# A two-layer transformer trunk on one core: transposes of the norm in four banks, buffers of their own for four weight units, gate/up blocks opened token tile by token tile, down projection in halves

## The chip, the core and the metric

The kernel runs on one core of a Trainium2 chip. Its engines work side by side, each on its own list of instructions in order: TensorE (PE) multiplies matrices into PSUM, which has eight banks of 128 x 512 float32; VectorE (DVE) and ScalarE (ACT) work element by element and empty PSUM; GpSimd (POOL) does small arithmetic and issues some DMAs; SyncE (SP) issues the DMAs that fetch weights. Semaphores hold an instruction back until what it reads is there and what it overwrites is free. The metric is the device time of one execution in microseconds (us); less is better.

## The reference, cut to what matters

256 tokens of width 2048 pass through two layers. After the attention of a layer:

```
x   = layer_norm(ALPHA * x + concat(out_a, out_b) @ w_o, ln1_g, ln1_b)
ffn = (silu(x @ w_gate) * (x @ w_up)) @ w_down          # 2048 -> 5632 -> 2048
x   = layer_norm(ALPHA * x + ffn, ln2_g, ln2_b)
```

All of it is float32. The attention part (a sparse head group with an indexer, and a latent head group) is not touched by the change.

## The kernel before, in words

**Weights.** A weight unit is 256 rows (two k of 128) by 512 columns, 512 KB. `load_unit` (L313) has SP fetch it into a `raw` buffer (L302), ACT copy it rounded into `wh` (L309) and DVE write the rest, raw minus wh, into `wl` (L310). A product is three matmuls of 512 columns for each k: high x high, high x low, low x high. Units go through 5 pairs of wh/wl, and 2 more in the phase called "more"; raw has 4 buffers and 2 more (`some`, L291). That phase lasts from the last pass of the output projection through the FFN to the first projection chunk of the next layer.

**Tokens.** There are two token tiles of 128, t0 and t1. `proj` (L317) takes a unit and multiplies both token tiles by it: 12 matmuls.

**Last passes.** `last_pass` (L772) ends the output projection, and the down projection likewise: eight units (4 columns of 512, two units each) are loaded, all of t0 is finished, then all of t1, so the units have to stay. After t0, and again after t1, `then` starts the norm of that token tile: `moments` (L360, bn_stats on DVE, two small POOL steps), `normalise`, and for the norms whose result is multiplied again `norm_T` (L381): four chunks of four 128 x 128 transposes on PE, each chunk read by four ACT instructions that apply the gain and the shift, then a copy and a subtraction on DVE that give the operands `xh` and `xl`. The chunks take PSUM banks 4 and 5 in turn. `norm_T` is a task that the loops advance: `tick()` after each unit lets tasks whose waiting is over emit their next step. The last norm of layer two is `norm_out` (L421), which writes the output.

**Gate and up.** The first of eleven blocks of 512 hidden columns is plain (`gu`, L809). In the other ten, `gate_up` (L852) does four quads: a quad is gate and up for one unit u and its partner u + 4. Quads 0 and 1 are plain: 4 units, 48 matmuls. Quads 2 and 3 are `wino_quad` (L887), a Strassen-Winograd form: 4 raw loads, 4 additions of raw units on DVE (L893), 7 products of 6 matmuls, each of which needs its own wh and wl; their token operands s1 to s4 come from `sum_operands` (L815) out of sums and differences of chunks 1 and 3 of the normalised tokens. Banks: c11 (gate, t0) 4, c21 (gate, t1) 5, c12 and c22 (up) 6 and 7 as one tile, the products p1, p5, p6, p7 in 0 to 3. At the end of the last wino quad eight DVE and ACT instructions put gate and up together (L904 to L933). The order is plain 0, `between`, wino 2, plain 1, wino 3. `hidden` (L831) then does silu, product, transposes and split into `hT`.

**Down.** `down` (L945) multiplies the hidden blocks two at a time. `between` in block 2 runs it for blocks 0 and 1: 4 columns of 4 units, 192 matmuls; block 4 does it for 2 and 3, and so on. Blocks 1, 3, 5, 7, 9 and 10 have no down in them. At the end come blocks 8 and 9, and block 10 as the last pass. From the third block on, results are added to x by a DMA with addition that POOL issues (L963).

**Order.** The source is one stream of instructions. The framework's planner deals them out to the engines: for each engine it takes, at every moment of a simulated run, the ready instruction that stands first in the source. So PE can run a later product while an earlier one waits for its weights; what is fixed by the plan then runs in that order on the chip. Tiles of one tag share its buffers; an instruction that writes a new tile waits until a buffer is free. The tag a8 has ten buffers of 8 KB per partition, for x, xh, xl, hT and the attention's outputs.

Of the kernel before, what the change touches and what calls it, by code (L numbers as in the profile page):

```python
# [31 lines left out]
P = 128  # L32
# [26 lines left out]
HALF = NKT // KU // 2  # L59
T2 = 11  # L60
LASTU = 2
# [17 lines left out]
def hybrid_trunk(ctx: ExitStack, tc: tile.TileContext, x, xt_in, pos, w_in, g_cq, g_ckv, w_uq,  # L79
# [225 lines left out]
    def parts(raw, n):  # L305
        pool, bufs = some("n", UNITS, MORE)
        wh = pool.tile([P, KU * C], F32R, name=nm("wh"), tag="wh", bufs=bufs)
        wl = pool.tile([P, KU * C], F32R, name=nm("wl"), tag="wl", bufs=bufs)
# [72 lines left out]
    def norm_T(gbT, y, hi, lo, keep=None):  # L381


        for _ in normalise(y, moments(y)):
            pass
        yield 5
        for c in range(D // C):
            tp = trp()
            transpose4([y[:, c * C + i * P:c * C + (i + 1) * P] for i in range(4)], tp)
            if keep is not None and c in keep:  # L390
                v = keep[c]
            else:
                v = t2([P, 4, P], "v")
# [84 lines left out]
    def layer(l, xh, xl, norms, last):  # L478
# [292 lines left out]

        def last_pass(unit, ks, lhs, then):  # L772

            us = [[load_unit(unit(c, k), KU * C) for k in ks] for c in range(D // C)]
# [24 lines left out]
        ffn, kept = [True], []  # L799
        phase["held"] = True  # L800
        for t in range(NT):
            v = phase["pool"].tile([P, 2, 4, P], F32, name=nm("kept"), tag="raw", bufs=RAWMORE)
            kept.append({1: v[:, 0], 3: v[:, 1]})
# [11 lines left out]
        def sum_operands():  # L815

            a = [[kept[t][c] for c in (1, 3)] for t in range(NT)]
            for name, x, y in (("s1", a[1][0], a[1][1]), ("s2", a[0][0], "s1"), ("s3", a[1][0], a[0][0]),
                               ("s4", a[0][1], "s2")):
                y = sums[y][2] if isinstance(y, str) else y  # L820
                v = t2([P, 4, P], "sv")
                nc.vector.tensor_tensor(v, x, y, op=ALU.subtract)
                hi, lo = (phase["pool"].tile([P, 4, P], F32R, name=nm(name), tag=name + p, bufs=1) for p in "hl")
                split(hi, lo, v)
                sums[name] = hi, lo, v
            phase["held"] = False

        def slhs(name):
            return lambda k: tuple(m[:, k % 4, :] for m in sums[name][:2])
# [22 lines left out]
        def gate_up(fc, plain, wino, between):  # L852
# [26 lines left out]
            def plain_quad(u, lastz):  # L879
                for i, col in enumerate(("c11 c21", "c12 c22")):  # L880
                    for v in (u, u + HALF):
                        w = load_unit(w_gu[i][l, fc, v], KU * C)
                        for t, name in enumerate(col.split()):
                            passes(name, token(t), unit(v), w, lastz and name == "c22" and v != u)
                        tick()

            def wino_quad(u, final):  # L887
# [11 lines left out]

                lo_, hi_ = unit(u), unit(u + HALF)  # L900
                p("p1", token(0), r11, lo_)
                if final:
                    e = t2([P, C], "e")
                    nc.scalar.activation(e, o["p1"], AF.Copy)  # L904
                p("p2", token(0), r21, hi_)
                if final:
                    g0 = t2([P, C], "g0")
                    nc.vector.tensor_tensor(g0, e, o["c11"], op=ADD)
# [6 lines left out]
                if final:  # L915
                    nc.vector.tensor_tensor(e, o["p6"], e, op=ALU.subtract)
                tick()
                p("p7", slhs("s3"), r12, lo_)
                if final:
                    v = t2([P, C], "v7")  # L920
                    nc.vector.tensor_tensor(v, e, o["p7"], op=ADD)
                    nc.vector.tensor_tensor(e, e, o["p5"], op=ADD)
                add(r21, r11, r21)
# [14 lines left out]
            for i, (u, w) in enumerate(zip(plain, wino)):  # L938
                plain_quad(u, i == len(plain) - 1)
                if i == 0:  # L940
                    between()
                r = wino_quad(w, i == len(wino) - 1)
            return r

        def down(fcs, hTs, then):  # L945
# [4 lines left out]
            units = C // P // KU * len(fcs)  # L950
            u0 = C // P // KU * fcs[0]
            if fcs[-1] == NFC - 1:
                units -= LASTU
            for c in range(D // C):
                o = proj([(w_down[l, c, u0 + u], range(u * KU, (u + 1) * KU)) for u in range(units)], lhs, C)
# [8 lines left out]
            if fcs[-1] == NFC - 1:  # L964
                finish(*[h[2] for h in held])
                last_pass(lambda c, k: w_down[l, c, u0 + k // KU], [(units + i) * KU for i in range(LASTU)], lhs, then)

# [15 lines left out]
        def group():  # L983
            finish(*[h[2] for h in held])
            if len(held) == 2 and held[-1][0] < NFC - 2:
                down([h[0] for h in held], [h[1] for h in held], behind_ffn)
                held.clear()

        g = gu(0, 0, lambda: finish(*norms))
        sum_operands()  # L990
        affine(ln1_g[l], ln1_b[l], 0)
        u = gu(1, 0)
        affine(ln1_g[l], ln1_b[l], 1)
        spawn_hidden(0, g, u, free_banks)
        for fc in range(1, NFC):
            g, u = gate_up(fc, (0, 1), (2, 3), group)
# [5 lines left out]
        ffn[0] = False  # L1002
# [4 lines left out]
        finish(*[h[2] for h in held[:2]])  # L1007
        down([h[0] for h in held], [h[1] for h in held], behind_ffn)
# [59 lines left out]
```

## Time and profile before

| | |
|---|---|
| median of 3 runs | 2224.64 us (2223.5 to 2225.68) |
| profiled execution, its own time | 2223.74 us |
| its span, first to last instruction | 2221.9 us |
| PE, DVE, ACT, POOL busy | 2179.9, 1699.9, 1191.0, 109.0 us |
| granted TensorE clock | 0.998 of full speed over the span |
| weights and the rest read from HBM | 416.33 MB |

Busy time counts an engine's instructions. Matmuls overlap: of two in a row the second starts before the first ends, so PE shows as busy without a break while they follow each other, and idle only where one starts late.

### The profile page before, as it was taken

To read this page: it belongs to the slowest core of one execution; us is meant where nothing else is said; L and a number is where in the kernel's file an instruction comes from. 1 tells how busy PE (TensorE), PEld (TensorE's weight loads), DVE (VectorE), ACT (ScalarE), POOL (GpSimd) and SP (SyncE) were. 2 spreads that over 40 slices of the span, in tenths; PEclk is the share of its full clock that TensorE was granted. 3 is DMA by queue.
4 is the path that set the end of the run, shared out by engine and by line. 5 is a ranking of instruction groups with operands and counts; after the bars stand their busy time and mean duration, and the time that the engine had idled before them with its cause. 6 is when DMAs were issued, how large, how long until landed. Compare 5 with 4: busy or idle time off the path is not lost. (4 is left out here: it accounts for less than half of the span.)

```text
span 2221.9 us, 27847 instructions
## 1 busy us (share of the span) xinstructions
PE 2179.9 (98%) x10128; PEld 1800.6 (81%) x10128; DVE 1699.9 (77%) x2215; ACT 1191.0 (54%) x1537; POOL 109.0 (5%) x198
## 2 busy tenths in 40 slices
PE   8999999999999999999999999999999999999997
PEld 7888888788788787877878888877888888888885
DVE  6685556987968788699567757568879697887985
ACT  5555544554545555565455554445545555555562
POOL 0100000100010000100100000000000100000002
PEclk9999999999999999999999999999999999999999
DMA  8544455665576766666755455547655758577583
GB/s 304 165 159 162 153 168 171 230 213 175 200 216 209 230 195 227 194 208 208 207 160 172 155 173 180 172 156 246 220 176 203 221 191 242 177 249 208 196 275 105
DMA packets 126057, 437.04 MB, mean 197 GB/s; under 512 B 14320, under 2 KB 14368, under 8 KB 125664
## 3 DMA queue, kind: packets, MB, share of 16 engines
q1 hardware_dynamic: 113760, 409.26, 54.9%
q0 software_dynamic: 12160, 26.01, 5.8%
q8 instruction: 79, 1.29, 0.2%
q14 instruction: 58, 0.48, 0.1%
HBM read 416.33 MB, written 2.10 MB: 188 GB/s over the span
## 5 line engine op out<-in xcount | busy, mean ns | idle before, releaser
L310 DVE TENSOR_TENSOR wl<-raw,wh 128x1024 fp32r<-128x1024 f32 (+1 forms) x892 | 1071.4, 1217 | 450.1 <-ACT wh L309 443.2
L309 ACT ACTIVATE wh<-raw 128x1024 fp32r<-128x1024 f32 (+1 forms) x892 | 926.3, 1055 | 844.6 <-PE acc L333 379.6
L331 PE MATMUL acc<-wh,xh 128*128 128x512 f32 (+1 forms) x768 | 302.5, 395 | 6.4 <-ACT wh L309 6.4
L332 PE MATMUL acc<-wl,xh 128*128 128x512 f32 (+1 forms) x768 | 297.8, 388 | 3.6 <-DVE wl L310 3.6
L333 PE MATMUL acc<-wh,xl 128*128 128x512 f32 (+1 forms) x768 | 297.1, 387 | 0.0
L331 PE MATMUL acc<-wh,hT 128*128 128x512 f32 x640 | 249.2, 390 | 0.8 <-ACT wh L309 0.4
L333 PE MATMUL acc<-wh,hT 128*128 128x512 f32 x640 | 249.2, 389 | 0.0
L332 PE MATMUL acc<-wl,hT 128*128 128x512 f32 x640 | 249.2, 389 | 0.0
L893 DVE TENSOR_TENSOR raw<-raw,raw 128x1024 f32<-128x1024 f32 x160 | 195.1, 1223 | 9.9 <-DMA raw<-in_w_up_dram 6.8
L868 PE MATMUL gu_c<-wh,xh 128*128 128x512 f32 x480 | 187.6, 391 | 7.8 <-DVE g L927 6.2
L870 PE MATMUL gu_c<-wl,xh 128*128 128x512 f32 x480 | 187.2, 390 | 0.0
L871 PE MATMUL gu_c<-wh,xl 128*128 128x512 f32 x480 | 186.9, 389 | 0.0
L331 PEld LDWEIGHTS acc<-wh,xh 128*128 128x128 f32 x768 | 144.3, 188 | 37.8 <-ACT wh L309 7.2
L332 PEld LDWEIGHTS acc<-wl,xh 128*128 128x128 f32 x768 | 144.7, 188 | 32.1 <-DVE wl L310 6.1
L333 PEld LDWEIGHTS acc<-wh,xl 128*128 128x128 f32 x768 | 144.5, 188 | 27.8
L331 PEld LDWEIGHTS acc<-wh,hT 128*128 128x128 f32 x640 | 120.1, 188 | 27.3 <-ACT wh L309 1.5
L333 PEld LDWEIGHTS acc<-wh,hT 128*128 128x128 f32 x640 | 120.2, 188 | 25.0
L332 PEld LDWEIGHTS acc<-wl,hT 128*128 128x128 f32 x640 | 120.1, 188 | 24.6
L868 PE MATMUL att<-wh,xh 128*128 128x512 f32 x320 | 127.7, 399 | 0.4 <-DVE e L933 0.3
L871 PE MATMUL att<-wh,xl 128*128 128x512 f32 x320 | 125.0, 391 | 0.0
L870 PE MATMUL att<-wl,xh 128*128 128x512 f32 x320 | 125.0, 391 | 0.0
L868 PEld LDWEIGHTS gu_c<-wh,xh 128*128 128x128 f32 x480 | 90.0, 188 | 29.7 <-DVE g L927 9.0
(241 smaller groups left out, 3002.6 us busy)
## 6 DMA issues: line engine op xcount, KB each, us to landing
raw<-in_w_gate_dram SPq DMA_DIRECT2D x176, 512.0 KB, 4.8
raw<-in_w_up_dram SPq DMA_DIRECT2D x176, 512.0 KB, 4.7
raw<-in_w_down_dram SPq DMA_DIRECT2D x176, 512.0 KB, 4.7
raw<-in_w_in_dram SPq DMA_DIRECT2D x144, 512.0 KB, 3.5
raw<-in_w_o_dram SPq DMA_DIRECT2D x64, 512.0 KB, 3.3
x<-d POOLq DMA_DIRECT2D x64, 256.0 KB, 6.5
raw<-in_w_in_dram SPq DMA_DIRECT2D x16, 400.0 KB, 3.1
raw<-in_w_uq_dram SPq DMA_DIRECT2D x12, 512.0 KB, 3.3
```

The costliest lines, as they stand in the source:

```text
L309: nc.scalar.activation(wh[:, :n], raw[:, :n], AF.Copy)
L310: nc.vector.tensor_tensor(wl[:, :n], raw[:, :n], f(wh[:, :n]), op=ALU.subtract)
L331: mm(o[t][:, :n], h, a, start=first, stop=False)
L332: mm(o[t][:, :n], h, b, start=False, stop=False)
L333: mm(o[t][:, :n], l, a, start=False, stop=final)
L868: mm(o[name], h, a, start=name not in begun, stop=False)
L870: mm(o[name], h, b, start=False, stop=False)
L871: mm(o[name], l, a, start=False, stop=end)
L893: nc.vector.tensor_tensor(d, x, y, op=ADD)
```

## The change

- `norm_T` uses four banks: 4, 5 and the pair 6, 7. t0's transposes start six units after its norm, not five. The chunks 1 and 3 are no longer kept in raw buffers for `sum_operands`; that now adds `xh` and `xl` up again (four more DVE additions) and runs after the second projection of block 0, not after the first. While chunks were kept, raw had only its 4 buffers; now 6 in the whole phase.
- `last_pass` gives four of its eight units wh and wl of their own: two in a tile of tag `many` (which later holds s1 to s4), two in a8.
- In a block's first quad both units of a column are loaded first and t0 is done for both, then t1.
- The instructions that empty the banks at the end of a block are raised by 60 places in the order (`sooner`), and those that don't free c11 or c21 come after the last product.
- `down` for blocks 0 and 1 is split: columns 0 and 1 behind the first quad of block 2, columns 2 and 3 behind that of block 3; blocks 2 and 3 in 4 and 5, and so on. Columns 2 and 3 of blocks 8 and 9 come after block 10, then the last pass.

```diff
-        if phase["name"] == "more" and not (key == "raw" and phase.get("held")):
+        if phase["name"] == "more":
...
-    def parts(raw, n):
-        pool, bufs = some("n", UNITS, MORE)
...
+    def parts(raw, n, own=None):
+        if own is not None:
+            wh, wl = own[:, 0], own[:, 1]
+        else:
+            pool, bufs = some("n", UNITS, MORE)
...
-        yield 5
+        yield wait
+        pair = att()
         for c in range(D // C):
-            tp = trp()
+            tp = trp() if c < 2 else pair[:, c - 2, :]
...
-            us = [[load_unit(unit(c, k), KU * C) for k in ks] for c in range(D // C)]
+            us = []
+            two = many([P, 2, 2, KU * C])
+            for c in range(D // C):
+                own = two[:, c] if c < 2 else t8([P, 2, KU * C], F32R, "own")
+                us.append([load_unit(unit(c, ks[0]), KU * C), parts(load_raw(unit(c, ks[1]), KU * C), KU * C, own)])
...
-            norms.append(spawn(norm_T(gbT, xt[t], xh[t], xl[t], kept[t] if ffn[0] else None)))
+            norms.append(spawn(norm_T(gbT, xt[t], xh[t], xl[t], 5 if t else 6)))
...
+            for k0, n, where in ((4, 4, many([P, 4, 2, 4, P])),):
+                a = {}
+                for t in range(NT):
+                    for i in range(2):
+                        ks = slice(k0 + i * NKT // 2, k0 + i * NKT // 2 + n)
+                        v = a[t, i] = t2([P, n, P], "av")
+                        nc.vector.tensor_tensor(v, f(xh[t][:, ks, :]), f(xl[t][:, ks, :]), op=ALU.add)
...
+                    vs = (u, u + HALF)
+                    ws = [load_unit(w_gu[i][l, fc, v], KU * C) for v in vs] if first else [None, None]
+                    for a in range(2):
+                        for b in range(2):
+                            t, j = (a, b) if first else (b, a)
+                            if ws[j] is None:
+                                ws[j] = load_unit(w_gu[i][l, fc, vs[j]], KU * C)
+                            name = col.split()[t]
+                            passes(name, token(t), unit(vs[j]), ws[j], lastz and i == 1 and a == b == 1)
...
+                def sooner():
+                    return tc.high_priority(offset=SOONER)
...
                 p("p4", token(1), r21, hi_)
                 if final:
-                    g1 = t2([P, C], "g1")
-                    nc.vector.tensor_tensor(g1, o["c21"], v, op=ALU.subtract)
-                    nc.vector.tensor_tensor(v, v, o["p5"], op=ADD)
-                    nc.vector.tensor_tensor(v, v, o["c22"], op=ADD)
+                    with sooner():
+                        g1 = t2([P, C], "g1")
+                        nc.vector.tensor_tensor(g1, o["c21"], v, op=ALU.subtract)
                 tick()
                 p("p3", slhs("s4"), r22, lo_)
                 if final:
+                    nc.vector.tensor_tensor(v, v, o["p5"], op=ADD)
+                    nc.vector.tensor_tensor(v, v, o["c22"], op=ADD)
+                    nc.vector.tensor_tensor(e, e, o["p5"], op=ADD)
                     nc.vector.tensor_tensor(e, e, o["c12"], op=ADD)
...
+                down(held[:2], (0, 1) if fc % 2 == 0 else (2, 3))
+                if fc % 2:
+                    del held[:2]
...
         g = gu(0, 0, lambda: finish(*norms))
-        sum_operands()
         affine(ln1_g[l], ln1_b[l], 0)
         u = gu(1, 0)
+        sum_operands()
...
+        down(held[:2], (2, 3))
+        finish(held[2][2])
+        u0 = C // P // KU * (NFC - 1)
+        last_pass(lambda c, k: w_down[l, c, u0 + k // KU], [0, KU], down_lhs([held[2][1]]), behind_ffn)
```

## Rows read from the trace of the kernel before

**Rows 1.** Busy time of the engines over the span, share, instructions.
```profile
PE 2179.9 (98%) x10128; PEld 1800.6 (81%) x10128; DVE 1699.9 (77%) x2215; ACT 1191.0 (54%) x1537; POOL 109.0 (5%) x198
```

**Rows 2.** Windows by stage: us, busy us (instructions) of PE, PEld, DVE, ACT, POOL, clock.
```profile
362.00:404.00 42.00, 39.19 (x184) 31.06 (x183) 34.49 (x55) 22.34 (x43) 3.72 (x5) 1.00 0.45 148
436.00:491.00 55.00, 54.38 (x246) 44.38 (x245) 49.38 (x54) 30.98 (x33) 0.00 (x0) 1.00 0.53 173
491.00:1042.00 551.00, 543.93 (x2409) 445.43 (x2408) 452.76 (x439) 299.61 (x322) 20.59 (x24) 1.00 0.64 205
1085.00:1126.00 41.00, 38.08 (x179) 30.26 (x179) 31.51 (x50) 21.09 (x42) 5.26 (x6) 1.00 0.45 131
1470.00:1515.00 45.00, 41.80 (x195) 32.94 (x194) 37.38 (x59) 24.28 (x46) 5.85 (x8) 1.00 0.50 156
1515.00:2150.00 635.00, 631.90 (x2817) 520.99 (x2816) 536.27 (x529) 351.63 (x379) 27.14 (x36) 1.00 0.66 214
```

**Rows 3.** Timeline, layer one's first norm: start, us, instruction, [idle before <- releaser].
```profile
373.80 1.06 ACT L309 ACTIVATE wh<-raw 128x1024 fp32r<-128x1024 f32 x1 [9.16 <-PE acc L784]
382.85 1.11 PE L351 MATMUL tr<-ident,x 128*128 128x128 f32 x8 [0.49 <-DVE x L378]
387.13 0.68 DVE L787 TENSOR_TENSOR x<-x,acc 128x512 f32<-128x512 f32 x1
390.54 1.06 POOL L369 TENSOR_SCALAR bnve<-bnmv 128x1 f32<-128x1 f32 x1 [8.34 <-DVE bnmv L366]
391.59 0.50 PE L332 MATMUL acc<-wl,xh 128*128 128x512 f32 x1 [1.22 <-DVE wl L310]
392.59 1.92 DVE L378 TENSOR_SCALAR x<-x,bnmv,bnrs 128x512 f32<-128x512 f32 x4 [0.46 <-POOL bnrs L370]
395.46 0.33 PE L351 MATMUL tr<-ident,x 128*128 128x128 f32 x1 [1.10 <-ACT v L396]
```

**Rows 4.** Waits of PE, both layers' gate/up blocks: total us, times, longest.
```profile
PE gu_c L868 <- DVE g L927: 3.5, 3, 1.5
PE att L868 <- DVE v L929: 1.7, 4, 0.5
PE gu_c L868 <- ACT wh L309: 1.6, 1, 1.6
...
PE gu_c L868 <- DVE g L927: 2.7, 3, 1.2
```

**Rows 5.** Windows: blocks 2 to 3, and a whole down projection.
```profile
536.00:607.00 71.00, 71.00 (x318) 58.49 (x317) 64.55 (x63) 40.70 (x43) 0.00 (x0) 1.00 0.57 188
620.00:664.00 44.00, 44.00 (x196) 36.43 (x195) 25.24 (x22) 20.46 (x24) 5.20 (x6) 1.00 0.71 205
```

**Rows 6.** Timeline, DVE and PE from the end of block 3.
```profile
607.08 1.22 DVE L310 TENSOR_TENSOR wl<-raw,wh 128x1024 fp32r<-128x1024 f32 x1
608.81 0.68 DVE L927 TENSOR_TENSOR g<-gu_c,v 128x512 f32<-128x512 f32 x1
609.55 0.50 PE L868 MATMUL gu_c<-wh,xh 128*128 128x512 f32 x1 [1.50 <-DVE g L927]
```

**Rows 7.** Window of blocks 0 and 1, columns as in rows 2.
```profile
404.00:491.00 87.00, 86.38 (x387) 70.64 (x386) 78.70 (x88) 50.48 (x55) 4.74 (x9) 1.00 0.67 224
```

**Rows 8.** Timeline, the end of the kernel.
```profile
2196.05 1.06 ACT L309 ACTIVATE wh<-raw 128x1024 fp32r<-128x1024 f32 x1 [9.28 <-PE acc L784]
2206.71 0.39 PE L784 MATMUL acc<-wh,hT 128*128 128x512 f32 x1
2208.33 0.68 DVE L787 TENSOR_TENSOR x<-x,acc 128x512 f32<-128x512 f32 x1
2209.77 0.26 DVE L366 BATCH_NORM_AGGREGATE bnmv<-bnst 128x2 f32<-128x24 f32 x1
2210.72 0.21 POOL L369 TENSOR_SCALAR bnve<-bnmv 128x1 f32<-128x1 f32 x1
```

**Rows 9.** DMAs that add down's results to x, 2140 to 2222 us.
```profile
DMA to landing us min/median/max: 3.3/5.5/8.8
```

More of the change, by code (lines that the diff above doesn't have):

```diff
@@ L59 @@
 HALF = NKT // KU // 2
+SOONER = 60
 T2 = 11
-LASTU = 2
 QI0, TA, QI1, TB, KA0, QA0, VA0, KA1, QA1, VA1 = range(10)
@@ L379, in normalise, with norm_T @@
             yield c, sl
-    def norm_T(gbT, y, hi, lo, keep=None):
+    def norm_T(gbT, y, hi, lo, wait):
         for _ in normalise(y, moments(y)):
             pass
-        yield 5
+        yield wait
+        pair = att()
         for c in range(D // C):
-            tp = trp()
+            tp = trp() if c < 2 else pair[:, c - 2, :]
             transpose4([y[:, c * C + i * P:c * C + (i + 1) * P] for i in range(4)], tp)
[L390 to L393, printed above, removed]
+            v = t2([P, 4, P], "v")
             for i in range(4):
@@ L815, in sum_operands @@
         def sum_operands():
[L817 to L826, printed above, removed]
+            for k0, n, where in ((4, 4, many([P, 4, 2, 4, P])),):
[5 more added lines that the diff above has]
+                        nc.vector.tensor_tensor(v, f(xh[t][:, ks, :]), f(xl[t][:, ks, :]), op=ALU.add)
+                prev = {}
+                for i, (x, y) in enumerate((((1, 0), (1, 1)), ((0, 0), "s1"), ((1, 0), (0, 0)), ((0, 1), "s2"))):
+                    v = prev[f"s{i + 1}"] = t2([P, n, P], "sv")
+                    nc.vector.tensor_tensor(v, a[x], prev[y] if isinstance(y, str) else a[y], op=ALU.subtract)
+                    hi, lo = where[:, i, 0], where[:, i, 1]
+                    split(hi, lo, v)
+                    for k in range(n):
+                        sums[f"s{i + 1}", k0 + k] = hi[:, k, :], lo[:, k, :]
         def slhs(name):
-            return lambda k: tuple(m[:, k % 4, :] for m in sums[name][:2])
+            return lambda k: sums[name, k]
         def hidden(gs, us, hT, tr):
@@ L850, in layer, with gate_up @@
         INTO = {"p2": "c11", "p4": "c21", "p3": "c12"}
-        def gate_up(fc, plain, wino, between):
+        def gate_up(fc, order, between):
             o, begun = {}, set()
@@ L877, in unit, with plain_quad @@
                 return range(u * KU, (u + 1) * KU)
-            def plain_quad(u, lastz):
+            def plain_quad(u, first, lastz):
                 for i, col in enumerate(("c11 c21", "c12 c22")):
[L881 to L884, printed above, removed]
+                    vs = (u, u + HALF)
[7 more added lines that the diff above has]
+                            passes(name, token(t), unit(vs[j]), ws[j], lastz and i == 1 and a == b == 1)
                         tick()
@@ L936, in wino_quad, with down_lhs @@
                     return [g0, g1], [e, v]
-            for i, (u, w) in enumerate(zip(plain, wino)):
-                plain_quad(u, i == len(plain) - 1)
+            lastp = max(i for i, q in enumerate(order) if q[0] == "plain")
+            for i, (kind, u) in enumerate(order):
+                if kind == "plain":
+                    plain_quad(u, i == 0, i == lastp)
+                else:
+                    r = wino_quad(u, i == len(order) - 1)
                 if i == 0:
                     between()
-                r = wino_quad(w, i == len(wino) - 1)
             return r
-        def down(fcs, hTs, then):
+        def down_lhs(hTs):
             def lhs(t, k):
@@ L948, in lhs, with down @@
                 return h[:, 0, j, t * P:(t + 1) * P], h[:, 1, j, t * P:(t + 1) * P]
[L950 to L955, printed above, removed]
+            return lhs
+        def down(pair, cols):
+            fcs, hTs = [h[0] for h in pair], [h[1] for h in pair]
+            finish(*[h[2] for h in pair])
+            per = C // P // KU
+            for c in cols:
+                o = proj([(w_down[l, c, per * fcs[0] + u], range(u * KU, (u + 1) * KU))
+                          for u in range(per * len(fcs))], down_lhs(hTs), C)
                 for t in range(NT):
@@ L963, in down @@
                         nc.gpsimd.dma_start(sl, d, accum_op=ALU.add)
-            if fcs[-1] == NFC - 1:
-                finish(*[h[2] for h in held])
-                last_pass(lambda c, k: w_down[l, c, u0 + k // KU], [(units + i) * KU for i in range(LASTU)], lhs, then)
         def behind_ffn(t):
@@ L981, in free_banks, with behind_quad, go @@
             return bank(2 + t, "tr")
[L983 to L987, printed above, removed]
+        def behind_quad(fc):
+            def go():
+                if fc < 2:
+                    return finish(*[h[2] for h in held])
+                down(held[:2], (0, 1) if fc % 2 == 0 else (2, 3))
+                if fc % 2:
+                    del held[:2]
+                finish(*[h[2] for h in held])
+            return go
+        ORDER = [("plain", 0), ("wino", 2), ("plain", 1), ("wino", 3)]
         g = gu(0, 0, lambda: finish(*norms))
-        sum_operands()
         affine(ln1_g[l], ln1_b[l], 0)
         u = gu(1, 0)
+        sum_operands()
         affine(ln1_g[l], ln1_b[l], 1)
@@ L995, in layer @@
         for fc in range(1, NFC):
[L996 removed]
+            g, u = gate_up(fc, ORDER, behind_quad(fc))
             if fc == 1:
```

35 lines of the change are left out of this document (16 added, 19 removed).

## The prediction

> **What bounds the kernel now.** I read the busy shares first: PE is busy for 98% of the span, DVE for 77%, ACT for 54% [rows 1]. The change leaves every matmul in place, so the most it can save is the time in which PE stands still. Next come the windows by stage, where a window's length less PE's busy time is PE's idle time [rows 2]. Around the three norms whose result is multiplied again it is 42 - 39.19 = 2.81, 41 - 38.08 = 2.92 and 45 - 41.80 = 3.20, together 8.93 us. In the gate/up blocks it is 0.62 and 7.07 in layer one and 3.10 in layer two, together 10.79 us. A wait costs a little more than its idle time: a down of 192 matmuls and four transposes takes 44 us [rows 5], 0.227 us a matmul, while one alone shows as 0.39 us [rows 8], so after a pause 0.16 us of overlap is missing too. Third, the timeline and the table of waits say what ends each pause.
>
> At a norm there are three: for the normalised x, for a `wl`, and for ACT that still reads one of the two transpose banks [rows 3]. In the blocks PE waits for the emptying of c21 (g, 3.5 and 2.7 us in the two layers), for that of c12 and c22 (1.7) and for a wh (1.6) [rows 4]. In the timeline they stand at the ends of blocks without a down: from 536 to 607 us, which holds the end of block 2 with its down, PE is busy for 71.00 of 71 us [rows 5], and at the end of block 3, which has none, it stops for 1.50 us [rows 6]. The reason is DVE. A plain quad asks 4 x 1.22 = 4.9 us of it for 48 x 0.227 = 10.9 us of PE, a wino quad 11 x 1.22 = 13.4 us for 42 x 0.227 = 9.5 us. A block without down costs DVE 36.6 us, with its eight emptying and four `hidden` instructions of 0.68 us about 45, and PE only 41. A down is where DVE catches up: 25.24 busy of 44 us [rows 5].
>
> **The change, part by part.**
>
> *Own buffers and the four banks (the norms).* Seven pairs can't hold eight units, so the eighth waits until t1 has used the first: ACT stands still for 9.16 us before it can split it [rows 3], and t0's last column, with its norm, comes after t1's first ones. With four pairs of their own all eight units fit, t0 is complete 4 x 2.73 = 10.9 us after the pass begins, and its norm lies under t1's 10.9 us of matmuls. The pause for t0's x (0.49 and its like) goes. The pause for ACT on a bank goes with four banks: four ACT readings take 1.5 us, and chunk three no longer waits for chunk one. The `wl` pause (1.22) came from DVE doing both norms at once, with no free pair ahead; now three pairs are free and two more raw buffers are in use. What can be late next is t1's norm. From its last x addition at 387.13 to the end of normalising at 392.59 + 1.92 it took 7.4 us [rows 3], with weight splits between; PE has five units of t0 alone for it, 5 x 6 x 0.227 = 6.8 us, so it comes 0.6 us late by that row. From both sides: with no split in between the chain is some 4.8 us and nothing is lost; with three more splits of 1.22 it ends 2.9 us late less what the transposes cover. I take 1.2 us left at each norm, for t1 and for t0's first chunk together. Three norms: 8.93 + 9 x 0.16 = 10.4 now, 3.6 after, a gain of 6.8 (bounds 1.7 and 10.4).
>
> One row speaks against: POOL's first norm step took 1.06 us beside a weight split [rows 3], against 0.21 us at the end of the kernel, where no split runs [rows 8]. The Trainium skill's SBUF page (SBUF — State Buffer, Who interferes with whom) says why: a VectorE instruction with two SBUF inputs and a GpSimd one that reads SBUF share a port, and the later one is blocked until the other is done. By that rule a split may hold back either POOL step in full, and the sum at its worst is the 2212 of the last rival below, not 2206. The trace agrees for the first step: 0.85 us of one split.
>
> *First quad by token tile, banks emptied earlier, down in halves (the blocks).* From block 2 on every block gets half a down (8 units, 96 matmuls, 22 us of PE, of which DVE is idle for half of 44 - 25.24, 9.4 us [rows 5]) behind its first quad. Every block end then follows a down, as that of block 2 does now, which loses nothing [rows 5]. A block then asks some 45 + 9.8 = 55 us of DVE in 62.7 us of PE. Raising the emptying puts g right behind its product, where it now stands behind a split of 1.22 us and another emptying (607.08 to 608.81, and PE goes on at 609.55 [rows 6]), and c21 is first written 6 matmuls, 1.36 us, later. The price is that the second weight unit of a block is wanted 1.36 us earlier, and that in DVE's list the splits for the last product and for the next block's units now stand behind a g that waits for PE: if PE is later than planned, they are late by up to that product, 1.36 us, and PE waits for them. The blocks lose 10.79 + 14 pauses x 0.16 = about 13 us now. Block 1 still has no down; its end (0.62 us idle and its overlap, 0.9) stays, and I leave 1.0 for the rest. Gain 11 (bounds 4 and 13).
>
> On SP nothing is added: the same 512 KB units are fetched, eight from w_down per block where there were sixteen in every second. POOL issues the same number of additions to x, behind each half. The last one must have landed before the last pass adds to that column of t0, 10.9 us after the pass begins. ACT's copy (about 0.9 us after the half) and at most 8.8 us to landing [rows 9] make 9.7; covered, by 1.2 us.
>
> *The sums.* Four more additions of 512 columns at 0.68 us, as DVE's others take [rows 3, 6], 2.7 us of DVE per layer, and all of sum_operands moves from behind the first projection to behind the second, so that it must be ready within a plain quad and two products. DVE has 87 - 78.70 = 8.3 us idle there [rows 7], and t0's norm now leaves it earlier. Bounds 0 and 2.7 us per layer; I charge 0.5, nearer to 0 because DVE's idle time there is three times the extra: 1.0 in all.
>
> *The end.* The same early t0 helps the last norm: ACT waits 9.28 us before the eighth unit [rows 8], so t0's output work lies after the matmuls and t1's last x addition starts at 2208.33, though its matmul started at 2206.71 and ended at 2207.10. With t0 done earlier it starts at about 2207.2: 1.1 us. POOL's step for t1 then waited for its four additions for t0, 2210.72 after a bnmv that ended at 2209.77 + 0.26 [rows 8]: 0.7 us. Gain 1.8 (bounds 0.5 and 2.5); what follows is unchanged.
>
> *Sum.* 6.8 + 11 + 1.8 - 1.0 = 18.6 us off the profiled execution's 2223.74, 2205.1. The median of the runs is 0.9 us above it, so 2206.
>
> **The rivals.**
>
> *DVE stays the bound at the block ends (2211).* Emptying earlier and wanting the second unit earlier only changes which DVE result PE waits for, from g to a wl. For it: DVE shows no gap through block 3's end. Against it: the ends of blocks with a down. Half of the blocks' gain goes: 2206 + 5.5.
>
> *The change doesn't do what it says (2215).* The two own pairs in a8 need buffers at a moment when x (2), the attention's outputs (2), xh and xl (4) are live too: exactly ten of ten. If one comes free late, the eighth unit waits as now; the norms keep their 10.4 us and the end its 1.8: 2206 + 6.8 + 1.8.
>
> *Half a down is too short (2230, slower).* One mechanism: DVE's backlog from a block is not worked off in half a down, and every block end pauses as those of the odd ones do now, 20 ends where there are 10. That adds 13 us where the forecast takes off 11; with the other terms, 2224.64 + 13 - 6.8 - 1.8 + 1.0 = 2230. It decides where a half's 9.4 us of idle DVE is less than what a block without down asks too much, 45 - 41 = 4 us and the pauses' 2; there is room of 3 us.
>
> *POOL's steps are blocked in full (2212).* If both steps of t1's chain wait for a whole split at every norm, 2 x 1.22 us come on top of the chain; three norms make some 6 of the 6.8 us disappear. Against it: the row has 0.85 us on the first step alone, and the end of the kernel none [rows 3, 8]. This is the rule of the Trainium skill's SBUF page above, taken at its worst.
>
> **How the numbers follow.** Forecast 0.56 (own range 2200 to 2212), DVE the bound 0.2, not what it says 0.1, POOL blocked 0.07, half too short 0.07. A measurement of this kernel tells some 0.2%, 4.4 us, from no change: faster means below 2220.2, slower above 2229.1. All but the last rival lie below 2220; allowing for two of them together I put faster 0.85, within 0.09, slower 0.06. If every bounded term goes well the gain is 25 us, 2199; at the poor ends it is 1.7 + 4 + 0.5 - 5.4, nearly nothing. The range 2198 to 2219 leaves two in ten out, most of it above.
>
> **What would show it.** In the changed kernel's windows by stage, PE's idle time should be about 1 us at each of the three norms and below 0.3 us at every block end but block 1's; no ACT wait of 9 us in the last passes; t1's last x addition within 0.2 us of its matmul's end. PE waiting for wl L310 at block ends in place of g shows the first rival; a wait for an s before p5 in block 1 shows that the sums cost more; a stop at each of the twenty block ends would make the forecast wrong as a whole.

## The result and the profile after

The changed kernel takes 2195.80 us in the median of 4 runs (2193.86 to 2196.59); the kernel before, 2224.62 us. The ratio is 0.9865, 95% interval 0.9853 to 0.9878: 28.8 us off. The forecast of 2206 had the sign right and the size wrong: the gain is 10 us larger, and the time lies below the range of 2198 to 2219. The profiled execution took 2193.86 us, with a span of 2191.9, 30.0 less than before.

The busy line of the changed kernel, as in [rows 1]:

```profile
PE 2169.4 (99%) x10128; PEld 1804.3 (82%) x10128; DVE 1709.0 (78%) x2223; ACT 1196.7 (55%) x1537; POOL 103.9 (5%) x198
```

PE's busy time fell by 10.5 us, though the same 10128 matmuls ran. So a good third of the gain was never idle time by this view. The windows by stage (us, then busy us and instructions of PE, PEld, DVE, ACT, POOL, then clock) answer to [rows 2] and [rows 7]; they are moved by what has been saved up to each:

```profile
363.00:405.00 42.00, 42.00 (x200) 34.06 (x199) 34.66 (x56) 19.81 (x41) 3.64 (x8) 1.00 0.45 145
433.00:488.00 55.00, 55.00 (x253) 45.65 (x252) 49.42 (x55) 31.82 (x34) 0.00 (x0) 1.00 0.50 168
488.00:1025.00 537.00, 537.00 (x2401) 444.90 (x2400) 446.36 (x430) 299.85 (x322) 24.07 (x28) 1.00 0.67 213
1069.00:1110.00 41.00, 41.00 (x196) 33.31 (x195) 31.90 (x51) 21.33 (x43) 3.35 (x6) 1.00 0.40 122
1446.00:1491.00 45.00, 45.00 (x214) 36.55 (x213) 36.44 (x58) 21.45 (x42) 2.87 (x6) 1.00 0.47 156
1491.00:2120.00 629.00, 629.00 (x2817) 521.80 (x2816) 529.61 (x520) 354.08 (x378) 30.06 (x39) 1.00 0.67 214
```

PE is never idle at the three norms, in layer one's blocks, or in layer two's up to 2120 us. One wait of PE is left in layer two; before, the tables behind [rows 4] count 14 in both layers, as the prediction does:

```profile
PE acc L335 <- DVE e L958: 1.6, 1, 1.6
```

A busy share can't tell where the time went, so I compared start times of the same matmul, by its number in the list, which is the same stage in every variant. In the profiled executions, us against before:

| | norm 1 | blocks, layer 1 | norm 2 and attention | norm 3 | blocks, layer 2 | end |
|---|---|---|---|---|---|---|
| before, us | 73.29 | 649.49 | 383.95 | 73.82 | 641.70 | 36.96 |
| changed | -3.7 | -13.5 | -3.3 | -4.2 | -4.3 | -2.0 |
| changed, run again | -3.7 | -13.5 | -3.3 | -4.3 | -1.8 | -2.0 |

(The first column is a norm and block 0; what comes ahead of it varies by up to 1.6 us between the profiles here.) The three norms gave 11.2 us, not 6.8; the blocks 17.9, not 11; the end 2.0, as the term of 1.8 had it. In the second profile of the same kernel only layer two's blocks differ, by 2.6 us; the last experiments are about that, and until then a difference of that size in layer two's column says nothing about a part.

The timeline of the first norm, answering to [rows 3]:

```profile
376.20 1.06 ACT L313 ACTIVATE wh<-raw 128x1024 fp32r<-128x1024 f32 x1 [9.52 <-PE acc L794]
376.65 0.24 POOL L373 TENSOR_SCALAR bnve<-bnmv 128x1 f32<-128x1 f32 x1 [271.42 <-DVE bnmv L370]
382.81 0.60 PE L355 MATMUL tr<-ident,x 128*128 128x128 f32 x4
388.79 0.67 DVE L797 TENSOR_TENSOR x<-x,acc 128x512 f32<-128x512 f32 x1
391.85 0.26 POOL L373 TENSOR_SCALAR bnve<-bnmv 128x1 f32<-128x1 f32 x1 [14.32 <-DVE bnmv L370]
392.80 1.92 DVE L382 TENSOR_SCALAR x<-x,bnmv,bnrs 128x512 f32<-128x512 f32 x4 [0.76 <-POOL bnrs L374]
394.42 0.60 PE L355 MATMUL tr<-ident,x 128*128 128x128 f32 x4
```

ACT still waits 9.5 us, but now ahead of a unit that only the next projection wants. t0's norm runs at 376 us beneath t1's matmuls, and neither tile's transposes (382.81, 394.42) show idle time ahead of them. From t1's last addition to the end of normalising it is 5.9 us, less than the 6.8 that PE has in t0's units.

The end of block 3, DVE and PE, answering to [rows 6]:

```profile
602.23 0.68 DVE L952 TENSOR_TENSOR g<-gu_c,v 128x512 f32<-128x512 f32 x1
602.83 1.21 DVE L314 TENSOR_TENSOR wl<-raw,wh 128x1024 fp32r<-128x1024 f32 x1
605.14 0.39 PE L879 MATMUL gu_c<-wh,xh 128*128 128x512 f32 x1
```

g ends at 602.91. By the order of the source the matmul at 605.14 is the first to write c21 again, behind twelve for t0: where PE stood still for 1.50 us, there are now 2.2 us to spare. The end of the kernel, answering to [rows 8]:

```profile
2178.44 0.39 PE L794 MATMUL acc<-own,hT 128*128 128x512 f32 x1
2178.87 0.69 DVE L797 TENSOR_TENSOR x<-x,acc 128x512 f32<-128x512 f32 x1 [0.31 <-PE acc L794]
2180.32 0.27 DVE L370 BATCH_NORM_AGGREGATE bnmv<-bnst 128x2 f32<-128x24 f32 x1
2180.67 0.22 POOL L373 TENSOR_SCALAR bnve<-bnmv 128x1 f32<-128x1 f32 x1 [1.64 <-DVE bnmv L370]
```

The last x addition starts 0.04 us after its matmul ends, where it was 1.2 us late, and POOL's step 0.08 us after its input.

### The profile page after: what moved, and what is told of

Read it like the earlier page. It is cut to its first block, busy times and chain, and to the rows that moved or that the text cites. A ratio compares the mean times of both kernels' runs of the same rounds, so it can differ in the third digit from the quotient of the medians.

```text
span 2191.9 us, 27923 instructions
## 1 busy us (share of the span) xinstructions
PE 2169.4 (99%) x10128; PEld 1804.3 (82%) x10128; DVE 1709.0 (78%) x2223; ACT 1196.7 (55%) x1537; POOL 103.9 (5%) x198
## 5 line engine op out<-in xcount | busy, mean ns | idle before, releaser
L313 ACT ACTIVATE wh<-raw 128x1024 fp32r<-128x1024 f32 (+1 forms) x876 | 916.2, 1056 | 792.2 <-PE acc L337 350.4
L314 DVE TENSOR_TENSOR wl<-raw,wh 128x1024 fp32r<-128x1024 f32 (+1 forms) x876 | 1050.6, 1216 | 379.8 <-ACT wh L313 368.0
L911 DVE TENSOR_TENSOR raw<-raw,raw 128x1024 f32<-128x1024 f32 x160 | 195.7, 1224 | 21.9 <-DMA raw<-in_w_up_dram 17.9
L995 POOL DMA_DIRECT2D x<-d x64 | 55.1, 879 | 1202.0 <-ACT d L994 697.0
```

Source lines behind the costliest of these rows:

```text
L911: nc.vector.tensor_tensor(d, x, y, op=ADD)
L995: nc.gpsimd.dma_start(sl, d, accum_op=ALU.add)
```

## The experiments

Each kernel undoes or does one part or a group of them. Each ratio is to the kernel before in the same session, where its median lay between 2224.37 and 2226.58 us, so compare ratios rather than times. The stage columns are those of the table above, from one profile of each kernel. "Order" means where the instructions that empty the banks stand at the end of a block.

### Which part carries the blocks: halves, order or first quad

Undoing the halves alone in the changed kernel:

```
-                down(held[:2], (0, 1) if fc % 2 == 0 else (2, 3))
-                if fc % 2:
-                    del held[:2]
                 finish(*[h[2] for h in held])
+                if len(held) == 2 and held[-1][0] < NFC - 2:
+                    down(held[:2], range(D // C))
+                    held.clear()
...
-        down(held[:2], (2, 3))
+        down(held[:2], range(D // C))
```

> The changed kernel with whole down projections again, behind the first quad of blocks 2, 4, 6 and 8 and after block 10; the rest of the change stays. The changed kernel's blocks became 17.9 us shorter (13.5 in layer one, 4.3 in layer two). Theory A (halves: DVE's backlog is worked off in every block): the blocks lose some 16 us again, time about 2212 us, with stops of PE at the ends of blocks 3, 5, 7 and 9. Rival B (order: c21 emptied earlier and wanted later): they lose under 2 us, time 2196 to 2198.

Undoing the order (with the raise), and the same with the old first quad too:

```
-                    with sooner():
-                        g1 = t2([P, C], "g1")
-                        nc.vector.tensor_tensor(g1, o["c21"], v, op=ALU.subtract)
+                    g1 = t2([P, C], "g1")
+                    nc.vector.tensor_tensor(g1, o["c21"], v, op=ALU.subtract)
+                    nc.vector.tensor_tensor(v, v, o["p5"], op=ADD)
+                    nc.vector.tensor_tensor(v, v, o["c22"], op=ADD)
                 tick()
                 p("p3", slhs("s4"), r22, lo_)
                 if final:
-                    nc.vector.tensor_tensor(v, v, o["p5"], op=ADD)
-                    nc.vector.tensor_tensor(v, v, o["c22"], op=ADD)
...
-                    plain_quad(u, i == 0, i == lastp)
+                    plain_quad(u, False, i == lastp)
```

> The changed kernel with the old emptying order and no raise; the first quad by token tile and the halves stay. Theory E: as slow as with the first quad undone too, about 2208 us, p3 waiting for v at each block end. Rival F, if the first quad carries it: 2199 at most.

> The changed kernel with the old emptying order, without the raise by 60 places, and with the old first quad (both token tiles for each unit); the halves stay. Theory A (halves): at most 2 us slower, 2196 to 2198. Rival B (order): the blocks lose 16 us again, about 2212 us, waits for g at the block ends.

The first quad alone, and the raise alone (every `with sooner()` taken off):

> The changed kernel with the old first quad (both token tiles for each unit); the new emptying order and the raise stay. Theory E: at most 2 us slower, 2196 to 2198. Rival F: some 6 us, 2202, waits for g at the block ends.

> The changed kernel without the raise by 60 places; emptying order, first quad and halves stay. Theory E: at most 2 us slower than the changed kernel, 2196 to 2198. Rival F: 6 us or more, 2202 at least, waits for g at the block ends.

| undone in the changed kernel | us | ratio to before | blocks, layer 1 | blocks, layer 2 |
|---|---|---|---|---|
| nothing | 2195.80 | 0.9865 [0.9853, 0.9878] | -13.5 | -4.3 |
| halves | 2197.71 | 0.9871 [0.9855, 0.9888] | -11.0 | -3.7 |
| order and raise | 2207.74 | 0.9926 [0.9910, 0.9943] | -3.7 | -2.0 |
| order, raise, first quad | 2209.27 | 0.9921 [0.9906, 0.9936] | -2.3 | +0.5 |
| first quad | 2195.60 | 0.9870 [0.9856, 0.9885] | -12.0 | -2.1 |
| raise | 2193.32 | 0.9864 [0.9849, 0.9879] | -13.3 | -4.6 |

My theory of the halves falls here: without them the blocks lose 3.2 of 17.9 us, while without the order they lose 12.2 (in layer one alone 2.5 and 9.9). The raise shows no effect by itself. Without the first quad layer one is about 1.5 us longer in the profile (one stop of 1.1 us for an x of the down); in the medians nothing is seen of it. With the old order and the halves, PE stops in layer one for something else than g (waits of PE, order, raise and first quad undone):

```profile
PE att L879 <- DVE v L950: 2.7, 8, 0.3
PE att L879 <- DVE e L954: 0.2, 1, 0.2
```

The timeline of that kernel at the end of block 2, DVE and PE:

```profile
544.19 0.68 DVE L950 TENSOR_TENSOR v<-v,att 128x512 f32<-128x512 f32 x1
544.92 0.50 PE L879 MATMUL att<-wh,many 128*128 128x512 f32 x1 [0.35 <-DVE v L950]
```

And of the changed kernel in the same place:

```profile
537.38 0.39 PE L879 MATMUL att<-wh,many 128*128 128x512 f32 x1
...
541.48 0.68 DVE L957 TENSOR_TENSOR v<-v,att 128x512 f32<-128x512 f32 x1
542.08 0.68 DVE L959 TENSOR_TENSOR e<-e,att 128x512 f32<-128x512 f32 x1
```

c12 and c22 are two halves of one tile. In the old source `v += c22` stands ahead of the product p3, which writes c12, so the first matmul of p3 waits for that addition (544.92 after 544.19), and the plan puts 24 matmuls of the next block ahead of it. In the new source p3 comes first and waits for nothing (537.38), and both readings follow (541.48, 542.08).

### The order and the halves on the kernel before

If that is the mechanism, moving one line of the old kernel must show it:

```
-                    nc.vector.tensor_tensor(v, v, o["c22"], op=ADD)
                 tick()
                 p("p3", slhs("s4"), r22, lo_)
                 if final:
+                    nc.vector.tensor_tensor(v, v, o["c22"], op=ADD)
                     nc.vector.tensor_tensor(e, e, o["c12"], op=ADD)
```

> The kernel before with one line moved: at the end of a block, the addition that reads c22 stands behind the last product p3, not ahead of it. c12 and c22 are the two halves of one PSUM tile; p3 writes c12. Theory E (p3 is held back by the reading of c22, so PE has to do the next block's first column ahead of it, and DVE's list falls behind): the move alone gives most of the blocks' 17.9 us, some 12, about 2212 us. Rival F (c21 is emptied too late, for want of the raise and of the first quad by token tile): under 2 us, 2223 to 2225.

Then the whole new order without the raise, the halves alone, and both together, each on the kernel before:

> The kernel before with the new emptying order alone (c22 and both readings of p5 behind p3, the last weight sum ahead of v), no raise, old first quad, whole downs, shared pairs. Moving c22 alone gave 6.8 us in the blocks, undoing the order in the changed kernel cost 12.2. Theory E2 (g also comes too late because a reading of p5 stands ahead of it, and halves are worth some 3 us by themselves): blocks 12 to 14 us shorter, about 2211 us. Rival G (the order needs the halves: DVE is behind in blocks without a down): no more than c22 alone, 2217 to 2218.

> The kernel before with the down projection in halves alone. Undoing the halves in the changed kernel cost 3.2 us. Theory E2: with the old order p3 waits at every block end, so little, 0 to 4 us, 2220 to 2224. The prediction's own step (halves carry the blocks): 11 us, 2213. Its rival (half a down is too short): slower, 2230.

> The kernel before with two parts alone: the down in halves, and the new emptying order at the end of a block (without the raise). Theory B (the order takes away the wait of p3 for c22 and, with it, most stops; the halves remove the stops that are left at the ends without a down): the blocks of layer one lose 13 us of their 649.49, those of layer two 2 to 5, the norms stay within 1 us of before, in all 15 to 18 us off, 2207 to 2210. Theory A (what the order gives needs the own pairs and the four banks, which leave DVE less to do at a block's start): the blocks lose no more than the order alone gave, 10.8 us, in all 2214.

| done in the kernel before | us | ratio to before | blocks, layer 1 | blocks, layer 2 |
|---|---|---|---|---|
| reading of c22 behind p3 | 2217.91 | 0.9972 [0.9963, 0.9982] | -4.9 | -1.9 |
| whole new order | 2214.44 | 0.9953 [0.9938, 0.9967] | -8.7 | -2.1 |
| halves | 2222.47 | 0.9988 [0.9979, 0.9997] | -2.0 | +0.1 |
| new order and halves | 2208.24 | 0.9926 [0.9912, 0.9940] | -13.7 | -3.6 |

One line gives 6.8 us in the blocks, about half of what I expected of it, and p3 no longer waits for v. What PE waits for in its place is g, a new stop of 1.7 us for an hT ahead of a down, and twice an e (waits of PE, layer one):

```profile
PE gu_c L868 <- DVE g L927: 2.8, 3, 1.4
PE acc L331 <- DVE hT L355: 1.7, 1, 1.7
PE att L868 <- DVE e L933: 0.9, 2, 0.7
```

The whole order gives 10.8, a little short of the 12 to 14 expected; what then remains in layer one is the stop for g at the four block ends without a down (waits of PE, new order alone):

```profile
PE gu_c L868 <- DVE g L926: 3.1, 4, 1.3
```

The halves alone take those away and put the stop at p3 in their place (waits of PE, halves alone):

```profile
PE att L868 <- DVE v L929: 2.8, 8, 0.4
PE att L868 <- DVE e L933: 0.3, 1, 0.3
```

Order and halves together give 17.3 in the blocks, and the table of waits then has none of PE in layer one's blocks. So each part leaves the other's stop standing: 10.8 and some 2 alone, 17.3 together; in layer one, where no other stop comes in, 8.7 and 2.0 alone, 13.7 together. On top of the new order the halves are thus worth 6.5 us here, twice the 3.2 that undoing them costs in the changed kernel. There the whole downs bring no stop for g back, so another part of the change covers for the halves; which one isn't shown.

The halves also have a price of their own in layer two. In every kernel here with halves, save the last two below, PE stops for 1.8 to 2.9 us, from start to start, in the down behind the last block (for v, 2.4 us idle, with the halves alone); none of the kernels with whole downs has that stop. The last two experiments take it away.

### Which part carries the norms

Shared pairs for all eight units again, and the transposes in banks 4 and 5 again:

```
-            us = []
-            two = many([P, 2, 2, KU * C])
-            for c in range(D // C):
-                own = two[:, c] if c < 2 else t8([P, 2, KU * C], F32R, "own")
-                us.append([load_unit(unit(c, ks[0]), KU * C), parts(load_raw(unit(c, ks[1]), KU * C), KU * C, own)])
+            us = [[load_unit(unit(c, k), KU * C) for k in ks] for c in range(D // C)]
```

> The changed kernel with the eight last units in the shared seven pairs again; four banks stay. The norms became 11.2 us shorter and the end 1.8. Theory C (the early t0 carries the norms): all of the end and two thirds of the norms come back, 1.8 + 7.5, about 2205 us, with the ACT wait of some 9 us before the eighth unit. Rival D (the four banks carry them): 1.8 + 2, about 2200 us.

```
-        pair = att()
         for c in range(D // C):
-            tp = trp() if c < 2 else pair[:, c - 2, :]
+            tp = trp()
```

> The changed kernel with norm transposes in banks 4 and 5 alone; own pairs stay. Theory C (the early t0 carries the norms): about 1.1 us at each of three norms for ACT's reading, 2199 us at most, end unchanged. Rival D (the banks carry them): 7 us, about 2203 us.

| undone | us | ratio to before | norm 1 | norm 2 | norm 3 | end |
|---|---|---|---|---|---|---|
| own pairs | 2208.02 | 0.9916 [0.9902, 0.9931] | -0.5 | +0.2 | -1.0 | 0.0 |
| four banks | 2194.95 | 0.9857 [0.9843, 0.9872] | -3.9 | -3.3 | -4.5 | -2.0 |

The norms' windows without own pairs, then with two banks:

```profile
362.00:404.00 42.00, 39.85 (x186) 31.26 (x185) 34.96 (x56) 21.37 (x42) 5.56 (x7) 1.00 0.49 159
1071.00:1112.00 41.00, 38.84 (x182) 30.41 (x181) 32.62 (x52) 21.72 (x43) 5.26 (x6) 1.00 0.40 125
1451.00:1496.00 45.00, 42.91 (x199) 33.77 (x198) 36.69 (x56) 24.01 (x44) 4.80 (x6) 1.00 0.51 162
```

```profile
363.00:405.00 42.00, 42.00 (x201) 34.34 (x200) 34.53 (x56) 20.81 (x41) 3.40 (x7) 1.00 0.42 134
1069.00:1110.00 41.00, 41.00 (x196) 33.48 (x195) 31.89 (x50) 20.83 (x42) 3.35 (x6) 1.00 0.38 120
1446.00:1491.00 45.00, 45.00 (x214) 36.85 (x213) 36.00 (x57) 22.00 (x43) 2.86 (x6) 1.00 0.44 147
```

Own pairs carry 9.9 of the norms' 11.2 us and all of the end; with them, two banks idle as little as four. But four banks are not useless by themselves. At the first norm t1's first transposes look like this without own pairs, then with two banks:

```profile
392.91 1.11 PE L355 MATMUL tr<-ident,x 128*128 128x128 f32 x8
393.91 0.63 PE L355 MATMUL att<-ident,x 128*128 128x128 f32 x4
```

```profile
394.50 0.60 PE L355 MATMUL tr<-ident,x 128*128 128x128 f32 x4
396.31 0.60 PE L355 MATMUL tr<-ident,x 128*128 128x128 f32 x4
```

Without own pairs the first three chunks follow each other at once, as the first two did before, and the third goes into bank 6 or 7 without the 1.10 us of waiting for ACT that it had [rows 3]. With own pairs the chunks come 1.8 us apart, matmuls between them, and two banks are read in time. So either part takes this pause away, and undoing the banks alone hides that. t0's later start and the two additional raw buffers were not undone by themselves.

All parts for the norms alone, on the kernel before with its order and its whole downs:

> The kernel before with the parts for the norms alone: own pairs for four units, four transpose banks, the sums of operands later; old emptying order, whole downs, old first quad. If the parts add up: norms 3.7 + 3.3 + 4.2 and the end 1.8 come off, the blocks stay within 1 us, in all 11 to 13 us, 2212 to 2214, and with the 15 to 18 us of the run beside it the whole 29 us of the change. If the parts need each other, the two runs together stay 3 us or more short of 29.

It took 2213.79 us, 0.9949 [0.9935, 0.9963]: norms -3.7, -3.3 and -4.3, end -2.0, blocks -0.6 and +3.6 (two stops for g of together 2.4 us in layer two, and smaller ones for a wh), where I expected them to stay within 1 us. By the medians 11.1 us here and 16.6 with order and halves are 27.7 of the change's 28.8: the two groups of parts add up within 1.2 us. By the profiles they come to 26.3 us, against 30.0 in the first profile of the change and 27.3 in the second.

### The stop that is left

The changed kernel once more as control, and with both readings of p5 right behind g in the last block:

```
                         nc.vector.tensor_tensor(g1, o["c21"], v, op=ALU.subtract)
+                        if fc == NFC - 1:
+                            nc.vector.tensor_tensor(v, v, o["p5"], op=ADD)
+                            nc.vector.tensor_tensor(e, e, o["p5"], op=ADD)
...
```

> The changed kernel once more, unchanged, to set beside the others on the same chip: 0.9865 of the kernel before within 0.001.

> The changed kernel, but in the last block, which a down follows at once, both readings of p5 stand right behind g1, as there the down's sums take p5's bank. The changed kernel stops for 1.6 us there in layer two. If that wait is on the path: 1.5 us faster than the changed kernel in the same comparison. If DVE is the bound there, the wait turns into one for a wl and the time is the same.

The control took 2196.05 us, 0.9868 [0.9851, 0.9884], the early readings 2195.03, 0.9865 [0.9850, 0.9880]. The stop stayed (e starts at 2137.02), but the edit tested nothing: the plan had both readings there already. In both kernels DVE's list runs g, one weight split, v and e with p5, then v and e with c22 and c12. PE's wait with the early readings:

```profile
PE acc L335 <- DVE e L955: 1.9, 1, 1.9
```

The last down begins on bank 0 in layer two, and its second token tile wants bank 1, where p5 lies. So the next kernel moves the down, not the readings; the one after it also leaves out the raise and two of the banks:

```
+        turns["acc"] = 1
         down(held[:2], (2, 3))
```

> The changed kernel with one line more: the down behind the last block always begins on accumulation bank 2, where in layer two it begins on bank 0 and so meets bank 1, still read as p5, with its second tile. Theory: the only stop left in the blocks, 1.6 to 2.3 us at 2135 us, with the stretch of matmuls at half the granted clock that follows it in some executions, goes: 1.7 to 4 us less than the changed kernel, 2191.5 to 2194. Rival: p7, on bank 3, is emptied as late as p5 in that block, or a wl comes late instead: a stop of 1 us or more stays at that place, and the time is that of the changed kernel, 2195 to 2196.

> The same with two things left out of the changed kernel that moved nothing alone: the raise by 60 places, and the two additional transpose banks. If they do nothing together either, it is within 1 us of the run above, 2190.5 to 2194; if either covers for the other, the norms or the block ends show stops again and it is 2 us or more slower.

2192.53 us (2191.59 to 2193.66), 0.9854 [0.9841, 0.9868], and 2191.98 (2191.27 to 2192.66), 0.9853 [0.9839, 0.9866]. In neither has the table of waits a line for PE in layer two's blocks. No run of either is as slow as the fastest of the changed kernel's first four (2193.86); against the control on the same chip in another session it is 3.5 and 4.1 us by the medians, which the intervals of the ratios don't separate by themselves. Kernels that keep the stop came near it in some runs (raise undone: median 2193.32, fastest 2192.85), so that the stop is gone is shown by the tables of waits, its worth only roughly by the times. The last kernel has the lowest median here, and it is the shorter one.

## Why the prediction was wrong, step by step

- **The norms.** The mechanism was right and lies in the own pairs. Mis-sized was "I take 1.2 us left at each norm": nothing is left, and the 11.2 us gained show that the 10.4 reckoned as lost there, the upper bound, were 0.8 too few. t1's chain takes 5.9 us, between the 4.8 without a split and the 7.4 of [rows 3]; POOL's first step took 0.26 us and not 1.06, since no weight split ran beside it. Without own pairs it took 1.07 and 1.06 again, each beside a split. The Trainium skill (SBUF — State Buffer, Who interferes with whom) says that a VectorE instruction with two SBUF inputs contends with a GpSimd one that reads SBUF; these traces agree, with 1.06 to 1.07 us beside a split and 0.24 to 0.26 without. The own pairs moved the splits away from the chain, so the rival "POOL's steps are blocked in full" found nothing to price. The four banks, which the prediction gave the pause for ACT, do end it where the own pairs are missing; with the own pairs t1's chunks come 1.8 us apart, and two banks are enough.
- **The blocks, the cause.** "The reason is DVE" and "Every block end then follows a down" was the step that failed. Undoing the halves costs 3.2 us, not 11, and on top of the new order in the kernel before they give 6.5; undoing the order costs 12.2. What held of it: the halves do take away the stops for g at the ends without a down. The row for the rest stood in front of me: [rows 4] has PE att waiting for v four times, 1.7 us, and I put it down to DVE's load alone. What made DVE's lateness count there was an order between two instructions that share a tile and no data. Moving the reading behind the product takes 6.8 us off with DVE's work unchanged.
- **The rival "half a down is too short".** Its sign was wrong, though its pattern was real: with the old order, halves make PE stop at most block ends, for v (eight waits of 0.3 to 0.4 us in layer one). At a third of a microsecond and not 1.3 each, that still left the halves alone 1.9 us ahead.
- **The blocks, the size.** The premise "the most it can save is the time in which PE stands still" failed, and with it "The blocks lose 10.79 + 14 pauses x 0.16 = about 13 us now", which missed a part. From start to start, gaps over 0.15 us beyond the usual pitch lose 10.0 us in layer one and 4.0 in layer two, close to the 13; but 78 smaller ones, of 0.02 to 0.15 us, lose another 6.9, and in the changed kernel 27 of them 2.4. That is 4.5 of the 6.9 us by which the blocks' gain came out larger than forecast. They are matmuls that start late while the one before still shows as running: no row of idle time has them. Of the 78, 54 stand directly behind a group of transposes or one matmul further on, and 16 are the second matmul behind a pause: after a pause not only the first matmul is late, but the next one too, by another 0.11 us. Why fewer are late behind transposes in the changed kernel isn't shown. The Trainium skill (Perfetto Trace Analysis, Identifying the Most-Contended Engine) says that matmul busy share is not a good measure of how close a kernel is to roofline, because pipelined instructions look smaller in the trace; this case agrees that it misleads, with busy time 10.5 us shorter for the same matmuls.
- **The sums** cost PE nothing that its idle time shows, where I charged 1.0: in layer one DVE is busy for 77.16 of 83 us between 405 and 488, against 78.70 of 87 [rows 7], and PE has no idle time in it.

```profile
405.00:488.00 83.00, 83.00 (x376) 68.85 (x375) 77.16 (x87) 49.86 (x54) 3.20 (x6) 1.00 0.61 206
```

- **The end** was right: 1.8 us behind the last matmul.

The rivals "DVE stays the bound" and "doesn't do what it says" fell with the windows. In the sum, 18.6 was forecast for a profiled execution that lost 30.0 us of span: short by 4.4 at the norms, 6.9 at the blocks, 1.0 for the sums and 0.2 at the end, less the 1.0 us by which the stages ahead of the first norm, which the change doesn't touch, ran longer in this execution.

## What to carry to other kernels

When a wait names an addition or a copy, ask first whether the waiting instruction needs its result or only follows it in the source on the same tile: here two halves of one tile were ordered as one, and such a wait goes by moving a line, without any work saved. Where an engine's instructions overlap, measure what a stage loses from start to start of the same instruction, since idle time leaves out every start that is late by less than the overlap. And parts hide each other, so do them alone as well as undo them: in layer one the order gave 8.7 us alone, the halves 2.0, and both 13.7, while in the changed kernel four transpose banks looked useless because the own pairs had taken away the same pause.

## What was not expected of the hardware

After the remaining stop, the same kernel ran on at two speeds. The windows around it in the control (columns as above; the clock stands after POOL):

```profile
2137.00:2139.00 2.00, 0.56 (x2) 0.46 (x3) 2.00 (x5) 1.07 (x2) 0.98 (x2) 0.91 0.90 340
2139.00:2141.00 2.00, 2.00 (x6) 1.53 (x5) 2.00 (x4) 1.06 (x1) 0.52 (x1) 0.50 0.69 176
2141.00:2146.00 5.00, 5.00 (x26) 4.18 (x24) 4.42 (x4) 2.71 (x3) 0.02 (x1) 0.89 0.92 279
```

Its stop lasted 2.94 us from start to start. After it the granted clock was 0.50, the 1.2 GHz level, and eight matmuls followed each other in 0.427 us where 0.227 is usual: 1.6 us more. In the run for the early readings the stop was 2.27 us, and the same eight followed. In the first profile of the changed kernel it was 1.95 us and the clock stayed at 1.00:

```profile
2139.00:2141.00 2.00, 2.00 (x10) 1.68 (x9) 2.00 (x4) 2.00 (x3) 0.54 (x1) 1.00 0.97 356
```

The longer stop and the slow stretch behind it, 1.0 and 1.6 us, make up the 2.6 us by which layer two's blocks differ between the two profiles of one kernel (-4.3 and -1.8). With the stop gone, the clock stayed at 1.00 through this place in both versions. The length of the stop alone doesn't tell which follows: at the same matmul the kernel before with order and halves stopped for 2.65 us and the clock stayed at 1.00, while with two banks 2.20 us were soon followed by seven matmuls 0.427 us apart.

Why the stop is 1.95 us in one execution and 2.94 in another shows in DVE's list ahead of it, in the first profile and then in the control:

```profile
2115.48 1.22 DVE L911 TENSOR_TENSOR raw<-raw,raw 128x1024 f32<-128x1024 f32 x1 [3.70 <-DMA raw<-in_w_up_dram]
2116.40 1.23 DVE L911 TENSOR_TENSOR raw<-raw,raw 128x1024 f32<-128x1024 f32 x1 [4.45 <-DMA raw<-in_w_up_dram]
```

In the last block DVE waits for a weight that is still being fetched, 0.75 us longer in the control. A second such wait (0.32 us against 0.26) and one for a wh (0.54 against 0.35) add 0.25, which makes the 1.0 us. Why the transfers land later in one execution than in the other stays open.
